# A transformer layer's two feed-forward blocks: one adding transfer, one reload and a few sums made at other places

## The chip, the cores and the metric

The kernel runs on one core of a Trainium2 chip. The metric is the device time of one execution in microseconds (us); lower is better. Three executions of the kernel before took 1108.47, 1108.53 and 1110.59 us, a median of 1108.53.

## What is computed

One layer of a streaming encoder for 512 tokens of width 1024 in float32: a feed-forward block (FFN 1), a mixer (a recurrent branch and windowed attention, joined by gates), and a second feed-forward block (FFN 2). The change touches the two feed-forward blocks alone. Cut to that:

```python
def swiglu(x, w1, w3, w2):
    return (jax.nn.silu(x @ w1) * (x @ w3)) @ w2

f = swiglu(rms_norm(h, ffn1_pre_g[l]), ffn1_w1[l], ffn1_w3[l], ffn1_w2[l])
h = h + 0.5 * rms_norm(f, ffn1_post_g[l])
...
f = swiglu(rms_norm(h, ffn2_pre_g[l]), ffn2_w1[l], ffn2_w3[l], ffn2_w2[l])
h = h + 0.5 * rms_norm(f, ffn2_post_g[l])
```

The hidden width is 2816, that is 22 slices of 128.

## The kernel before

**Precision.** PE multiplies in a short format. Every float32 operand is therefore split into two parts, hi (a rounded copy, by ACT) and lo (the operand less hi, mostly by DVE); `split2` (L211 to L214) does both. Each product is three matmuls: hi by hi, lo by hi, hi by lo. In the rows `whi` and `wlo` are the parts of a weight, and `uT`, `hx` and `hT` hold both parts of an activation.

**Two stages for each block.** Both replace a block matrix product of eight multiplications by one of seven, in which sums and differences of blocks are multiplied.

- `Pairs` computes `x @ w1` and `x @ w3`. Each *pair job* takes two slices of a weight. While job n is multiplied, the operands of job n+1 are prepared: POOL (in FFN 2; POOL and DVE in FFN 1) makes sums of weight blocks, S12 and S34 (L817 to L823), ACT and DVE split them. `late[n, k]` hangs further work on point k of job n. The product of the two halves, `hEO`, is the hidden activation.
- `Halves` computes the hidden activation times `w2` in seven products, m1 to m7, each over G groups of four hidden slices (G is 4 in FFN 1, 5 in FFN 2). A *unit* is one group of one product, twelve matmuls (L651 to L653). FFN 2's order is m1, m5, m2, m6, m3, m7, m4, so units 0 to 4 are m1, 10 to 14 m2, 15 to 19 m6, 20 to 24 m3.

**What sets the order around the change.** The program is written out in the order in which each engine executes it; nothing is reordered later. `Halves.prep` (L594 to L637) prepares a unit up to LEAD = 5 units ahead of its matmuls: it takes two buffers `whi` and `wlo`, has ACT copy the weight to hi (L618), makes lo, splits the activation into `uT` or `hx`, and then calls `sums`, which overwrites blocks in place for later products. There are three ways to make lo: DVE subtracts (L626); or ACT writes a negated copy of the weight (L620) and a DMA issued by POOL adds the weight from memory onto it (L621), as m2 does; or ACT writes a negated copy of hi and the DMA adds the weight from SBUF (L624), for the pairs in BY_ADD. The sums on the weights are named T1 (`b12` less `b11`, needed by m5) and T2, both by `T` (L548, on tiles `raw_w2a` or `raw_w2b`); the sum S1 on the activation is also for m5 (L551, on `hEO`). Each is one DVE instruction. `t1(i)` and `s1(i)` can be called early for a group; `sums` then skips them.

In FFN 2, T1 of groups 0 to 2 stands at `late[end - 2, 1]`, in the job before the last but one; in the trace these are three L548 in a row. S1 of the groups 0 to 3 is early there as well. In FFN 1 neither is early: T1 and S1 of a group stand behind the splits of m1's unit.

m3 uses `b22` again, which T2 has overwritten. In FFN 2 it is loaded a second time, by SP (L633), one DMA for each of five preparations from number `cast_at` on, which is 4 * 5 - 5 = 15. SP's queue is executed in order, and each DMA on it waits until its buffer is free.

Of the kernel before, what the change touches and what calls it, by code (L numbers as in the profile page):

```python
# [51 lines left out]
def hybrid_layer(ctx: ExitStack, tc: tile.TileContext, a: dict, out: bass.AP):  # L52
# [10 lines left out]
    def slot(shape, dt=F32, name="s"):  # L63
        uid[0] += 1
        return sb.tile(shape, dt, tag="slot", name=f"{name}_{uid[0]}")
# [9 lines left out]
    def f32(ap):  # L75
        return ap.bitcast(F32)
# [72 lines left out]
    def dma_to(n):  # L149
        while st["dma"] < min(n, len(order)):  # L150
            dma_one(st["dma"])
            st["dma"] += 1
# [11 lines left out]
    def split_to(n):  # L164
        while st["split"] < min(n, len(order)) and st["split"] not in paired:
            k = st["split"]
            dma_to(k + 1)
            r = raws.pop(k)
            if order[k] in BY_DMA:
                nm, i = order[k]  # L170
                pairs[k] = split_dma(r, a[nm][i * P : (i + 1) * P, :])
            else:
                hi = slot([P, D], F32R, name="whi")
                lo = slot([P, D], F32R, name="wlo")
                if order[k] in BY_POOL:
                    pool.tensor_copy(hi, r)
                else:
                    act.activation(hi, r, AF.Copy)
                dve.tensor_tensor(out=lo, in0=r, in1=f32(hi), op=ALU.subtract)
                pairs[k] = (hi, lo)  # L180
            st["split"] += 1
# [29 lines left out]
    def split2(hi, lo, src):  # L211

        act.activation(hi, src, AF.Copy)  # L213
        dve.tensor_tensor(out=lo, in0=src, in1=f32(hi), op=ALU.subtract)  # L214
# [276 lines left out]
    class Hidden:  # L491

        def __init__(self, seq):
            self.seq, self.f, self.t, self.done, self.eo = seq, {}, {}, 0, {}
# [21 lines left out]
    class Halves:  # L516
# [5 lines left out]
        def __init__(self, nm, hid, hooks, gs, names):  # L522
            self.nm, self.hid, self.hooks, self.gs, self.names = nm, hid, hooks, gs, names
            self.G = G = len(gs)
            self.loads = [(b, i) for bs in (("b11", "b12"), ("b22", "b21")) for i in range(G) for b in bs]
            if G > 4:
                self.loads[2 * G :] = [(b, i) for b in ("b22", "b21") for i in range(G)]
            self.cast_at = names.index("m3") * G - 5
            self.raw, self.ops, self.loaded, self.ready = {}, {}, 0, 0
            self.bank, self.c, self.accs, self.cast, self.did = {}, {}, {}, {}, set()  # L530

# [62 lines left out]
        def prep(self, n, load=True):  # L594

            G = self.G
            while self.ready < min(n, 7 * G):
                u = self.ready
                self.ready += 1
                m, i = self.names[u // G], u % G  # L600
                if load:
                    self.load(min(4 * G, 2 * G + (u if u >= U_SLOTS else u == 3) if G > 4 else 2 * G + 1 + u))
                b, odd, half = self.OPERANDS[m]
                again = m == "m3" and G > 4
                hi = self.cast.pop(i) if m == "m3" and not again else slot([P, 2, 512], F32R, name="whi")
                lo = slot([P, 2, 512], F32R, name="wlo")
                if u < U_SLOTS:
                    xs = slot([P, 2, 2, 256], F32R, name="hx")
                else:
                    xs = uT[:, :, (u + 1) % 8, :].rearrange("p e (j c) -> p e j c", j=2)  # L610
                if again:
                    split2(hi, lo, self.cast.pop(i))
                elif m == "m3":
                    act.activation(lo, f32(hi), AF.Copy, scale=-1.0)
                    pool.dma_start(out=lo, in_=self.src(b, i), accum_op=ALU.add)
                else:
                    src = self.raw[b, i]
                    act.activation(hi, src, AF.Copy)  # L618
                    if m == "m2":
                        act.activation(lo, src, AF.Copy, scale=-1.0)  # L620
                        pool.dma_start(out=lo, in_=self.src(b, i), accum_op=ALU.add)  # L621
                    elif G > 4 and (m, i) in BY_ADD:
                        act.activation(lo, f32(hi), AF.Copy, scale=-1.0)
                        pool.dma_start(out=lo, in_=src, accum_op=ALU.add)  # L624
                    else:
                        dve.tensor_tensor(out=lo, in0=src, in1=f32(hi), op=ALU.subtract)  # L626
                split2(xs[:, 0, :, :], xs[:, 1, :, :], self.x(i, odd, half))
                self.ops[u] = hi, lo, xs
                if self.cast_at <= u < self.cast_at + G:
                    n = u - self.cast_at  # L630
                    if G > 4:
                        self.cast[n] = slot([P, 2, 512], name=f"raw_{self.nm}")
                        sp.dma_start(out=self.cast[n], in_=self.src("b22", n))  # L633
                    else:
                        self.cast[n] = slot([P, 2, 512], F32R, name="whi")
                        pool.dma_start(out=self.cast[n], in_=self.src("b22", n))
                self.sums(m, i)  # L637
# [53 lines left out]
    def blocks(nm, hid, pairs, late, h_src, gs, names, marks):  # L691

        hooks = {u: [] for u in range(7 * len(gs))}

        def tail_tile(n):
            hid.to(n + 1)
            split_to(st["get"] + n + 1)

        def h_back(t):
            h[t] = slot([P, D], name="h")  # L700
            sp.dma_start(out=h[t], in_=h_src(t))

        for at_, fn in zip(marks, (lambda n: dma_to(st["get"] + n + 1), tail_tile, h_back)):
            for n, u in enumerate(at_):
                hooks[u].append(lambda n=n, fn=fn: fn(n))
        half = Halves(nm, hid, hooks, gs, names)
        pairs.more = lambda n: half.load((LOAD_PAIRS if len(gs) == 4 else LOAD_B)[n])
        ahead = lambda: half.prep(min(half.ready + 1, U_SLOTS))
        end = len(pairs.jobs) - 1
        late[end, 1], late[end, 2 if pairs.R is None else 3] = [ahead], [ahead]  # L710
        if pairs.R is None:
            late[end - 4, 1] = [lambda i=i: half.s1(i) for i in range(len(gs) - 1)]
            late[end - 3, 1] = [lambda: half.load(6)]
            late[end - 2, 1] = [lambda i=i: half.t1(i) for i in range(3)]
            late[end - 1, 2] = [lambda: half.prep(1, False)]
            late[end, 1] = []
        pairs.run(ahead, late)
        return half

# [539 lines left out]
    def to_uT(src, hh, th):  # L1259
        v = [uT[:, e, 4 * hh : 4 * hh + 4, th * 256 : th * 256 + 256] for e in range(2)]  # L1260
        split2(v[0], v[1], src)
        return uview(hh, th)
# [19 lines left out]
    def keep(u):  # L1282
        f, i = u // 2, u % 2
        if f not in kept:
            kept[f] = slot([P, 2, SEQ], name="kept")
        act.activation(kept[f][:, i, :], ps[u], AF.Copy)
# [34 lines left out]
    late = {(0, 1): [lambda: keep(2 * NC1 - 1)], (1, 1): [bias_in], (2, 3): [bias_parts], (3, 1): [bias_rows]}  # L1321
# [5 lines left out]

    h.clear()
    half = blocks("w2a", hid, pairs_a, late, lambda t: a["x"][t * P : (t + 1) * P, :], GS_A, NAMES_A, MARKS_A)
    X1 = pairs_a = late = None  # L1330
    for fn, at_ in zip((gate_kept, silu_kept, swiglu_kept), KEPT_AT):
# [5 lines left out]
    half = None  # L1337
# [415 lines left out]
    late = {(0, 1): [lambda: X2.update(t4=to_uT(tn[3], 0, 1)), tn.clear]}  # L1753
    pairs_b.prep(1, 1)

    half = blocks("w2b", hid, pairs_b, late, lambda t: h_scr[t], GS_B, NAMES_B, MARKS_B)
    X2 = pairs_b = None
    last_gemm("w2b", hid, half, "ffn2_post_g", 0.5)
# [106 lines left out]
```

## Time and profile before

| | us |
|---|---|
| median of three executions | 1108.53 |
| the profiled execution | 1108.97 |
| its span in the profile | 1107.2 |
| PE busy | 1096.0 |
| DVE busy | 934.2 |
| ACT busy | 680.1 |
| POOL busy | 407.0 |

The profile shows one execution, instruction by instruction. A row of the timeline has the start, the duration, the engine, the line in the kernel, the operation and the tiles, written as output<-inputs; in brackets, if there is any, the idle time just ahead of it and what ended it. PE is the matmul engine, DVE, ACT and POOL are the vector, scalar and GpSimd engines, SP issues most of the loads. "x3" means that three like instructions are put into one row. Successive matmuls overlap, so that their starts are closer together than their durations are long. PE's granted clock was 0.999 of full speed.

### The profile page before, as it was taken

How to read it: one execution, taken by the hardware profiler on the slowest of the kernel's cores; microseconds unless marked ns; L12 is line 12 of the kernel's file. 1: busy time of each engine (PE TensorE's matmuls, PEld its weight loads, DVE VectorE, ACT ScalarE, POOL GpSimd, SP SyncE). 2: the span in 40 equal slices, each digit the busy share in tenths (PEclk: the TensorE clock that was granted, in tenths of full speed). 3: DMA queues.
4: the chain of work that ended last, by engine and by line, in shares of the span. 5: the costliest groups of instructions: out<-in, count | busy, mean ns of one | idle time of the engine just before them, and what ended most of it. 6: DMA issues, size and time to landing. Idle time of an engine off the chain costs nothing.

```text
span 1107.2 us, 17988 instructions
## 1 busy us (share of the span) xinstructions
PE 1096.0 (99%) x6838; PEld 987.7 (89%) x6838; DVE 934.2 (84%) x1324; ACT 680.1 (61%) x1187; POOL 407.0 (37%) x333
## 2 busy tenths in 40 slices
PE   9999999999999999999999999999999999999997
PEld 8899999987888877899888888888999999998786
DVE  5988999999977978887678867767889899999985
ACT  7755556576747678756656654456455555567672
POOL 0143435602112423233556573010976655521000
PEclk9999999999999999999999999999999999999999
DMA  9325663467944542156222335452323323557742
GB/s 334 124 83 143 132 141 115 133 212 151 250 186 168 149 117 101 39 161 244 72 89 84 112 136 209 138 185 95 116 81 111 115 77 115 190 163 180 190 129 80
DMA packets 53205, 156.44 MB, mean 141 GB/s; under 512 B 5488, under 2 KB 7408, under 8 KB 53120
## 3 DMA queue, kind: packets, MB, share of 16 engines
q1 hardware_dynamic: 44128, 132.19, 35.4%
q0 software_dynamic: 8704, 22.59, 10.5%
q8 instruction: 53, 0.87, 0.3%
q10 hardware_dynamic: 288, 0.52, 0.1%
q14 instruction: 32, 0.26, 0.1%
HBM read 137.47 MB, written 13.62 MB: 136 GB/s over the span
## 4 chain that ended last, share of the span: by engine, by line
PE 89%; DVE 6%; ACT 3%; DMA 1%; issue 1%; DVEq 0%; SPq 0%; ACTq 0%
PE c L770 12%; PE c L771 12%; PE c L769 12%; PE f L224 9%; PE f L226 9%; PE f L225 9%; PE hw L652 5%; PE hw L653 5%; PE hw L651 5%; PE acc L244 1%; PE acc L242 1%; PE acc L243 1%; DVE wlo L214 1%; PE pt L1623 1%; DMA wlo<-in_w2b_dram 1%
## 5 line engine op out<-in xcount | busy, mean ns | idle before, releaser
L770 PE MATMUL c<-uT,wlo 128*128 128x256 f32 x516 | 146.1, 283 | 0.3 <-DVE wlo L214 0.3
L771 PE MATMUL c<-uT,whi 128*128 128x256 f32 x516 | 146.0, 283 | 0.0
L769 PE MATMUL c<-uT,whi 128*128 128x256 f32 x516 | 146.0, 283 | 0.0
L770 PE MATMUL c<-Xh,wlo 128*128 128x256 f32 x504 | 142.9, 284 | 0.7 <-DVE wlo L214 0.5
L769 PE MATMUL c<-Xh,whi 128*128 128x256 f32 x504 | 142.7, 283 | 0.0
L224 PE MATMUL f<-uT,whi 128*128 128x512 f32 (+1 forms) x368 | 136.4, 371 | 0.0
L225 PE MATMUL f<-uT,wlo 128*128 128x512 f32 (+1 forms) x368 | 134.8, 366 | 0.0
L226 PE MATMUL f<-uT,whi 128*128 128x512 f32 (+1 forms) x368 | 134.8, 366 | 0.0
L771 PE MATMUL c<-Xl,whi 128*128 128x256 f32 x456 | 129.0, 283 | 0.0
L214 DVE TENSOR_TENSOR wlo<-S,whi 128x1024 fp32r<-128x1024 f32 x86 | 118.4, 1377 | 5.9 <-POOL OL L1659 3.1
L213 ACT ACTIVATE whi<-S 128x1024 fp32r<-128x1024 f32 x86 | 88.5, 1055 | 33.5 <-DVE S L818 32.1
L770 PEld LDWEIGHTS c<-uT,wlo 128*128 128x128 f32 x516 | 99.0, 192 | 0.7 <-DVE wlo L214 0.5
L769 PEld LDWEIGHTS c<-uT,whi 128*128 128x128 f32 x516 | 99.0, 192 | 0.2
L771 PEld LDWEIGHTS c<-uT,whi 128*128 128x128 f32 x516 | 99.0, 192 | 0.0
L770 PEld LDWEIGHTS c<-Xh,wlo 128*128 128x128 f32 x504 | 96.7, 192 | 1.2 <-DVE wlo L214 1.2
L769 PEld LDWEIGHTS c<-Xh,whi 128*128 128x128 f32 x504 | 96.7, 192 | 0.3 <-issue 0.3
L771 PEld LDWEIGHTS c<-Xl,whi 128*128 128x128 f32 x456 | 87.5, 192 | 0.0
L652 PE MATMUL hw<-wlo,uT 128*128 128x512 f32 x220 | 86.0, 391 | 1.2 <-DMA wlo<-in_w2b_dram 1.1
L653 PE MATMUL hw<-whi,uT 128*128 128x512 f32 x220 | 86.0, 391 | 0.2
L651 PE MATMUL hw<-whi,uT 128*128 128x512 f32 x220 | 85.8, 390 | 0.0
L224 PEld LDWEIGHTS f<-uT,whi 128*128 128x128 f32 x368 | 69.4, 189 | 12.6 <-issue 1.4
L226 PEld LDWEIGHTS f<-uT,whi 128*128 128x128 f32 x368 | 69.4, 188 | 11.4
(440 smaller groups left out, 3183.3 us busy)
## 6 DMA issues: line engine op xcount, KB each, us to landing
raw_w2b<-in_w2b_dram SPq DMA_DIRECT2D x27, 512.0 KB, 4.5
raw_w2a<-in_w2a_dram SPq DMA_DIRECT2D x22, 512.0 KB, 4.3
raw_w1b<-in_w1b_dram SPq DMA_DIRECT2D x22, 512.0 KB, 4.2
raw_w3b<-in_w3b_dram SPq DMA_DIRECT2D x22, 512.0 KB, 4.4
raw_w3a<-in_w3a_dram SPq DMA_DIRECT2D x21, 512.0 KB, 4.4
raw_w1a<-in_w1a_dram SPq DMA_DIRECT2D x20, 512.0 KB, 4.5
raw_wg<-in_wg_dram SPq DMA_DIRECT2D x16, 512.0 KB, 4.2
h<-in_x_dram SPq DMA_DIRECT2D x8, 512.0 KB, 7.3
```

The costliest lines, as they stand in the source:

```text
L213: act.activation(hi, src, AF.Copy)
L214: dve.tensor_tensor(out=lo, in0=src, in1=f32(hi), op=ALU.subtract)
L224: pe.matmul(ps[:, c0:c1], wh[:, s], h_, start=k == 0 and c0 == 0, stop=False, skip_group_check=True)
L225: pe.matmul(ps[:, c0:c1], wl[:, s], h_, start=False, stop=False, skip_group_check=True)
L226: pe.matmul(ps[:, c0:c1], wh[:, s], l_, start=False, stop=k == KT - 1, skip_group_check=True)
L242: pe.matmul(acc[n], x[:, 0, c], wh[:, s], start=first, stop=False, skip_group_check=skip)
L651: pe.matmul(ps, xs[:, 0, j, c], hi[:, j, :], start=start and j == 0, stop=False, skip_group_check=True)
L652: pe.matmul(ps, xs[:, 0, j, c], lo[:, j, :], start=False, stop=False, skip_group_check=True)
L653: pe.matmul(ps, xs[:, 1, j, c], hi[:, j, :], start=False, stop=i == self.G - 1, skip_group_check=True)
L769: pe.matmul(ps, wh[:, s], xh, start=first, stop=False, skip_group_check=True)
L770: pe.matmul(ps, wl[:, s], xh, start=False, stop=False, skip_group_check=True)
L771: pe.matmul(ps, wh[:, s], xl, start=False, stop=k == 3, skip_group_check=True)
```

## The change

Four edits, in three functions.

1. `cast_at` for G = 5 becomes 4 * 5 - 3 = 17: m3's `b22` is reloaded in the preparations 17 to 21.
2. In FFN 2's m2 the lo of group 4 is made by DVE's subtraction (L626) in place of ACT's negated copy and the adding DMA. FFN 1 has four groups and keeps all its adding DMAs.
3. In FFN 2's pair jobs T1 is made early for groups 0 and 1 only. T1(2) is made at its own unit, by `sums`.
4. In FFN 1 (`pairs.R` is not None) S1(0) and S1(1) are made at point 1 of the pair jobs 5 and 9.

```diff
-            self.cast_at = names.index("m3") * G - 5
+            self.cast_at = names.index("m3") * G - (5 if G == 4 else 3)
...
-                    if m == "m2":
+                    if m == "m2" and i < 4:
                         act.activation(lo, src, AF.Copy, scale=-1.0)
                         pool.dma_start(out=lo, in_=self.src(b, i), accum_op=ALU.add)
...
-            late[end - 2, 1] = [lambda i=i: half.t1(i) for i in range(3)]
+            late[end - 2, 1] = [lambda i=i: half.t1(i) for i in range(2)]
             late[end - 1, 2] = [lambda: half.prep(1, False)]
             late[end, 1] = []
+        else:
+            late[5, 1].append(lambda: half.s1(0))
+            late[9, 1].append(lambda: half.s1(1))
```

Where instructions move, on DVE. Lines from 720 on have numbers that are higher by 3 in the changed kernel (L880 and L883 are the same line); the numbers in names are the program's buffers. The first place is FFN 2's pair job ahead of the last but one, before:

```order
L214 TENSOR_TENSOR w22_1918_10381<-raw_w3b19_1882_10126,w22_1918_10381 128x512
L548 TENSOR_TENSOR raw_w2b_1907_10280<-raw_w2b_1907_10280,raw_w2b_1906_10278 128x1024
L548 TENSOR_TENSOR raw_w2b_1909_10284<-raw_w2b_1909_10284,raw_w2b_1908_10282 128x1024
L548 TENSOR_TENSOR raw_w2b_1911_10288<-raw_w2b_1911_10288,raw_w2b_1910_10286 128x1024
L214 TENSOR_TENSOR wlo_1929_10444<-raw_w1b20_1899_10256,whi_1928_10443 128x1024
L214 TENSOR_TENSOR wlo_1931_10461<-S12_1919_10384,whi_1930_10460 128x1024
L880 TENSOR_TENSOR cc_1924_10395<-c_1927_10398,ct_1923_10394 128x256
```

The same place in the changed kernel:

```order
L214 TENSOR_TENSOR w22_1918_10381<-raw_w3b19_1882_10126,w22_1918_10381 128x512
L548 TENSOR_TENSOR raw_w2b_1907_10280<-raw_w2b_1907_10280,raw_w2b_1906_10278 128x1024
L548 TENSOR_TENSOR raw_w2b_1909_10284<-raw_w2b_1909_10284,raw_w2b_1908_10282 128x1024
L214 TENSOR_TENSOR wlo_1929_10443<-raw_w1b20_1899_10256,whi_1928_10442 128x1024
L214 TENSOR_TENSOR wlo_1931_10460<-S12_1919_10384,whi_1930_10459 128x1024
L883 TENSOR_TENSOR cc_1924_10395<-c_1927_10398,ct_1923_10394 128x256
```

The third L548, T1(2) on `raw_w2b_1911`, has gone from ahead of the two splits `wlo_1929` and `wlo_1931`. It now stands in the preparation of m1's unit 2, behind that unit's split of `hx` with two short instructions between it and unit 3's L626.

The second place is in m2, where the fifth group is prepared, before (`uT` from `hEO_1895` is that group's activation, `raw_w2b_1978` and `raw_w2b_1959` are T2 and another sum behind it):

```order
L551 TENSOR_TENSOR hEO_1829_9742<-hEO_1829_9742,hEO_1828_9741 128x2x256
L214 TENSOR_TENSOR uT_78<-hEO_1895_10244,uT_78 128x512
L548 TENSOR_TENSOR raw_w2b_1978_10812<-raw_w2b_1978_10812,raw_w2b_1960_10675 128x1024
L548 TENSOR_TENSOR raw_w2b_1959_10673<-raw_w2b_1978_10812,raw_w2b_1959_10673 128x1024
L551 TENSOR_TENSOR hEO_1895_10244<-hEO_1895_10244,hEO_1894_10243 128x2x256
```

And in the changed kernel:

```order
L551 TENSOR_TENSOR hEO_1829_9742<-hEO_1829_9742,hEO_1828_9741 128x2x256
L626 TENSOR_TENSOR wlo_2009_11016<-raw_w2b_1997_10925,whi_2008_11015 128x1024
L214 TENSOR_TENSOR uT_78<-hEO_1895_10244,uT_78 128x512
L548 TENSOR_TENSOR raw_w2b_1978_10812<-raw_w2b_1978_10812,raw_w2b_1960_10674 128x1024
L548 TENSOR_TENSOR raw_w2b_1959_10672<-raw_w2b_1978_10812,raw_w2b_1959_10672 128x1024
L551 TENSOR_TENSOR hEO_1895_10244<-hEO_1895_10244,hEO_1894_10243 128x2x256
```

The L626 that writes `wlo_2009` is new on DVE; all behind it stands one instruction later.

The third place is FFN 1's last pair job, where m1's first units are prepared, before:

```order
L626 TENSOR_TENSOR wlo_418_2743<-raw_w2a_391_2585,whi_417_2742 128x1024
L214 TENSOR_TENSOR hx_419_2744<-hEO_149_786,hx_419_2744 128x512
L548 TENSOR_TENSOR raw_w2a_392_2587<-raw_w2a_392_2587,raw_w2a_391_2585 128x1024
L551 TENSOR_TENSOR hEO_149_786<-hEO_149_786,hEO_150_787 128x2x256
L912 TENSOR_TENSOR cc_396_2594<-cc_396_2594,Rb_19_144 128x1024
L626 TENSOR_TENSOR wlo_422_2794<-raw_w2a_393_2589,whi_421_2793 128x1024
L214 TENSOR_TENSOR hx_423_2795<-hEO_217_1293,hx_423_2795 128x512
L548 TENSOR_TENSOR raw_w2a_394_2591<-raw_w2a_394_2591,raw_w2a_393_2589 128x1024
L551 TENSOR_TENSOR hEO_217_1293<-hEO_217_1293,hEO_218_1294 128x2x256
```

In the changed kernel both L551 are gone from there. The first now stands in pair job 5:

```order
L895 TENSOR_TENSOR cc_191_1057<-ct_190_1056 128x256
L214 TENSOR_TENSOR w22_201_1168<-raw_w3a9_171_923,w22_201_1168 128x512
L551 TENSOR_TENSOR hEO_149_786<-hEO_149_786,hEO_150_787 128x2x256
L214 TENSOR_TENSOR wlo_212_1213<-raw_w1a10_188_1052,whi_211_1212 128x1024
L915 TENSOR_TENSOR cc_191_1057<-cc_191_1057,Rb_19_144 128x1024
```

The second stands at the like place of pair job 9. On SP the order of the DMAs is unchanged; which buffers m3's reloads take, and so what they wait for, is different.

## Prediction

> **What bounds the kernel now.** I read the page's busy times first, then the waits of the matmul engine, then its rows one by one at the places that the change touches.
>
> ```profile
> span 1107.2 us, 17988 instructions
> PE 1096.0 (99%) x6838; PEld 987.7 (89%) x6838; DVE 934.2 (84%) x1324; ACT 680.1 (61%) x1187; POOL 407.0 (37%) x333
> ```
>
> PE is the bound: it is busy in 1096.0 of 1107.2 us, and the change removes no matmul. So it can win only what PE waits for today. The list of PE's waits is short; its longest entry inside the feed-forward blocks is this one:
>
> ```profile
> PE hw L652 <- DMA wlo<-in_w2b_dram: 1.1, 1, 1.1
> ```
>
> Ends of matmuls are modelled, so a short wait shows better as a gap between starts. In FFN 1's m5 the starts are normally 0.23 us apart (here L653, L651, L652 follow each other):
>
> ```profile
> 249.30 0.39 PE L651 MATMUL hw<-whi,uT 128*128 128x512 f32 x1
> 249.77 0.50 PE L652 MATMUL hw<-wlo,uT 128*128 128x512 f32 x1
> 250.37 0.50 PE L653 MATMUL hw<-whi,uT 128*128 128x512 f32 x1
> 250.71 0.39 PE L651 MATMUL hw<-whi,uT 128*128 128x512 f32 x1
> ...
> 252.78 0.39 PE L651 MATMUL hw<-whi,uT 128*128 128x512 f32 x1
> ...
> 253.85 0.50 PE L653 MATMUL hw<-whi,uT 128*128 128x512 f32 x1
> ```
>
> The first four rows have gaps of 0.47, 0.60 and 0.34, so 0.24 + 0.37 + 0.11 = 0.72 over the normal three. From 252.78 to 253.85 are 1.07 for two steps, 0.61 over. These two units alone lose 1.33 us, and what ends the gaps is DVE, which runs there without a break: its split of uT ends at 253.80, and PE goes on at 253.85.
>
> ```profile
> 253.11 0.69 DVE L214 TENSOR_TENSOR uT<-hEO,uT 128x512 fp32r<-128x512 f32 x1
> ```
>
> **FFN 1: two S1 leave DVE's run.** The run starts in the last pair job:
>
> ```profile
> 226.99 0.68 DVE L551 TENSOR_TENSOR hEO<-hEO,hEO 128x512 f32<-128x512 f32 x1
> ...
> 228.73 1.22 DVE L626 TENSOR_TENSOR wlo<-raw_w2a,whi 128x1024 fp32r<-128x1024 f32 x1
> ...
> 231.60 0.69 DVE L551 TENSOR_TENSOR hEO<-hEO,hEO 128x512 f32<-128x512 f32 x1
> ...
> 232.87 1.22 DVE L626 TENSOR_TENSOR wlo<-raw_w2a,whi 128x1024 fp32r<-128x1024 f32 x1
> ```
>
> Both L551 rows go. Each has 0.69 on the row, but the next instruction starts about 0.09 before the end of the one ahead, so a step is 0.60. ACT's halves of the splits limit how far DVE can move up:
>
> ```profile
> 227.35 1.05 ACT L618 ACTIVATE whi<-raw_w2a 128x1024 fp32r<-128x1024 f32 x1
> ...
> 230.23 1.05 ACT L618 ACTIVATE whi<-raw_w2a 128x1024 fp32r<-128x1024 f32 x1
> ```
>
> The split at 228.73 can't start before 228.40, so the first S1 gives 0.30 there and not 0.60. The one at 232.87 could start at 232.87 - 0.30 - 0.60 = 231.97, after ACT's end at 231.28, so the run is 0.90 early from there. Behind it DVE has no idle time until PE has caught up, and the last gap closes by as much: **-0.90**. Bounds: -0.30 if ACT or a load holds the second split too, -1.33 from PE's gaps.
>
> The same two S1 are added in pair jobs 5 and 9, each ahead of a split that waits for ACT:
>
> ```profile
> 103.97 1.23 DVE L214 TENSOR_TENSOR wlo<-raw_w1a,whi 128x1024 fp32r<-128x1024 f32 x1 [2.62 <-ACT whi L213]
> ...
> 144.29 1.23 DVE L214 TENSOR_TENSOR wlo<-raw_w1a,whi 128x1024 fp32r<-128x1024 f32 x1 [1.18 <-ACT whi L213]
> ```
>
> 0.69 fits into 2.62 and into 1.18: cost 0. That idle time is the cover; without it each would delay its split by 0.60. What lies between FFN 1 and FFN 2 moves with PE.
>
> **FFN 2's pair jobs: one T1 fewer ahead of two splits.** DVE's and POOL's rows, then PE's:
>
> ```profile
> 963.62 4.58 DVE L548 TENSOR_TENSOR raw_w2b<-raw_w2b,raw_w2b 128x1024 f32<-128x1024 f32 x3
> 968.13 2.31 DVE L214 TENSOR_TENSOR wlo<-raw_w1b,whi 128x1024 fp32r<-128x1024 f32 x1
> 970.37 2.31 DVE L214 TENSOR_TENSOR wlo<-S,whi 128x1024 fp32r<-128x1024 f32 x1
> ```
> ```profile
> 967.31 2.05 POOL L822 TENSOR_TENSOR S<-raw_w3b 128x512 f32<-128x512 f32 x1 [2.45 <-PE c L771]
> 969.44 2.15 POOL L823 TENSOR_TENSOR S<-S,raw_w3b 128x512 f32<-128x512 f32 x1
> ```
> ```profile
> 969.94 0.28 PE L769 MATMUL c<-uT,whi 128*128 128x256 f32 x1
> 970.50 0.39 PE L770 MATMUL c<-uT,wlo 128*128 128x256 f32 x1 [0.28 <-DVE wlo L214]
> 970.72 0.28 PE L771 MATMUL c<-uT,whi 128*128 128x256 f32 x1
> ...
> 971.91 0.28 PE L769 MATMUL c<-Xh,whi 128*128 128x256 f32 x1
> 972.73 0.39 PE L770 MATMUL c<-Xh,wlo 128*128 128x256 f32 x1 [0.54 <-DVE wlo L214]
> ```
>
> With 0.12 as the normal step of a 256-wide matmul, PE loses 0.44 before 970.50, 0.70 before 972.73, and 0.10 at each restart (970.50 to 970.72): 1.34 us. The third L548 is T1(2), 1.13 long, and the two splits right behind it end the waits. Without it the first split starts at 967.00, before POOL's addition at 967.31. In the rows the two engines take turns: ends come at 969.36 (POOL), 970.44 (DVE), 971.59 (POOL), 972.68 (DVE), about 1.1 apart, where an undisturbed split takes 1.2. If DVE has its turn first, its splits end at 968.2 and 970.4, and both waits go: **-1.34**. If the splits keep 2.31 each, they end 1.13 early, and PE wins 1.13. So the bounds of this step are 1.13 and 1.34; I take 1.34, because the alternating ends fit the rows one by one. The Trainium skill's page "SBUF — State Buffer", section "Who interferes with whom", calls the port that DVE and GpSimd share an exclusive lock and no split of bandwidth; by that rule the step gives 1.34, by a shared pace 1.13, and the rows' ends agree with the lock.
>
> What is late next is the next job's first split, with 0.38 to spare (981.47 less 981.09):
>
> ```profile
> 979.88 1.21 DVE L214 TENSOR_TENSOR wlo<-raw_w3b,whi 128x1024 fp32r<-128x1024 f32 x1
> ...
> 981.47 0.28 PE L770 MATMUL c<-uT,wlo 128*128 128x256 f32 x1
> ```
>
> POOL's additions wait for PE ahead of the gaps, so they don't move up, and DVE loses some of its lead to them again. By turns, POOL's last addition comes one DVE turn earlier, about 1.1, and DVE's next operation behind it as well: a lead of 1.1 by estimate, 0.24 less than PE's 1.34, inside the 0.38. If DVE had no lead left there, PE would keep only 0.38 of the 1.34.
>
> **FFN 2's m2: the fifth lo by DVE.** In the chain of waits and PE's rows:
>
> ```profile
> 1023.71 8.69 DMA wlo<-in_w2b_dram
> ```
> ```profile
> 1030.98 0.39 PE L651 MATMUL hw<-whi,uT 128*128 128x512 f32 x1
> 1032.44 0.50 PE L652 MATMUL hw<-wlo,uT 128*128 128x512 f32 x1 [1.07 <-DMA wlo<-in_w2b_dram]
> 1032.78 0.39 PE L653 MATMUL hw<-whi,uT 128*128 128x512 f32 x1
> ```
>
> Gaps 1.46 and 0.34 against 0.23: 1.23 + 0.11 = **-1.34**. The adding transfer goes with ACT's negated copy ahead of it; DVE instead makes the lo just ahead of uT's split of the same unit, in a stretch where its splits are done over three us before PE asks for them (3.23 at the least, below). What was behind the transfer on PE needs nothing later than that. Bounds: 0 if something else holds unit 14 as long, 1.34 from PE's rows.
>
> **What DVE then carries.** T1(2) is back at m1's unit 2, a little ahead of the first row here, and the new L626 stands in m2. From here to m3 DVE has no idle time:
>
> ```profile
> 991.55 1.23 DVE L626 TENSOR_TENSOR wlo<-raw_w2b,whi 128x1024 fp32r<-128x1024 f32 x1 [0.38 <-ACT whi L618]
> ...
> 1037.04 0.69 DVE L214 TENSOR_TENSOR uT<-hEO,uT 128x512 fp32r<-128x512 f32 x1
> ```
> ```profile
> 1040.96 0.39 PE L653 MATMUL hw<-whi,uT 128*128 128x512 f32 x1
> ```
>
> The idle 0.38 and the 0.08 of overlap take 0.46 of T1's 1.14; DVE falls 0.68 behind PE. The new L626 adds 1.14, PE's vanished stall 1.34: 3.16 in all. The smallest spare behind it is at unit 17: uT's split ends at 1037.73, PE starts at 1040.96, 3.23, of which 0.06 is the handover. So 3.17 is there for 3.16. DVE becomes the bound's equal; I cost it at nothing, with the upper bound that each us of more lag is a us of PE.
>
> **m3's reload** moves from units 15 to 19 to units 17 to 21 of the preparation.
>
> ```profile
> 1022.83 10.12 SPq L633 DMA_DIRECT2D raw_w2b<-in_w2b_dram  x5
> ```
> ```profile
> raw_w2b<-in_w2b_dram SPq DMA_DIRECT2D x27, 512.0 KB, 4.5
> ```
>
> The five stay in the same place on SP's queue, but by the buffers that they now take they wait for the ends of units 13 to 16, 2.7 us apart (twelve matmuls of 0.23). Unit 16 ends where unit 17 begins, at about 1040.5, less 2.7: the fifth is issued near 1037.8 and lands near 1042.3. It is used in unit 24, seven units behind unit 17, near 1057 in the new time. Cost 0, on ACT's and SP's queues too; the next loads on SP wait for unit 17 and 18 anyway.
>
> **Sum.** 0.90 + 1.34 + 1.34 = 3.58; I write 3.5, since the margin on DVE is 0.01. The profiled execution took 1108.97 (span 1107.2 and 1.77 around it), so 1105.5; the median shown is 0.44 lower, which gives 1105.0. I say **1105.2**.
>
> **Rivals.**
> - *FFN 1 gives 0.30.* ACT's splits or the loads hold DVE. Against it: ACT is 0.7 ahead at 231.28. Sum 2.98: 1105.8.
> - *DVE becomes the bound in m6 or m3.* For it: the margin of 0.01. If the idle time absorbs nothing of T1(2) or POOL takes some tenths, PE loses 0.3 to 1.0 at unit 17 or 20: sum 2.6 to 3.3, 1105.5 to 1106.1.
> - *The next pair job takes T1's gain back, and FFN 1 gives 0.30.* 0.38 + 0.30 + 1.34 = 2.02: 1106.7, no measurable difference. With the m2 lo alone working it is 1107.4.
> - *Slower: the reload.* If SP's five transfers wait for later units than I read, they and the loads behind them slide by 2.7 per unit. The fifth has 1057 less 1042.3, less 2.3 for both halves of its split, 12.4 to spare; slower than before needs 3.6 more, six units in all. That the spare is so large speaks against it; price at eight units: 21.6 - 12.4 - 3.6 = 5.6, 1114.
>
> **Chances.** Forecast 0.50; FFN 1's or DVE's rival, still faster, 0.20; two of them together or the third, within 0.2%, 0.20; slower 0.10. A difference of 0.2%, 2.2 us, is about what a measurement of this kernel tells from none. Low end: 3.58 with PE's full 1.33 in FFN 1, 4.0 below the median, 1104.5; high end: FFN 1's 0.90 or little else works, 1107.9.
>
> **What would show it.** Right: no gap over 0.1 at L652 in m2's last unit; starts 0.12 apart around T1's job; the last m5 gaps of FFN 1 short by 0.9 in sum. Wrong: a wait at L653 on uT in m6 or at L653 of m3's first unit (DVE is the bound), a wait at the next pair job's first L770, a wait on raw_w2b at m3, or L770 waiting in jobs 6 or 10 of FFN 1.

## The result, and the profile after

Ten executions of each kernel: 1108.82 us before (1107.82 to 1111.33), 1106.43 us changed (1105.54 to 1108.23). The ratio is 0.9976, 95% interval 0.9966 to 0.9986: 2.4 us faster. The forecast was 1105.2, in a range of 1104.5 to 1107.9: the measured time lies in it, 1.2 us above the forecast. Of this 1.2, 0.3 is the starting point: the forecast set out from 1108.53, the median of three executions, and the median of ten is 1108.82. The profiled execution of the changed kernel has a span of 1104.3, against 1107.2, that is 2.9 us less. From its page:

```profile
span 1104.3 us, 17988 instructions
PE 1094.8 (99%) x6838; PEld 987.0 (89%) x6838; DVE 935.9 (85%) x1325; ACT 679.3 (62%) x1186; POOL 404.3 (37%) x332
```

One instruction more on DVE, one less on ACT and on POOL, as the order showed. Lines from 720 on are numbered higher by 3 here, so L772 to L774 are the L769 to L771 of before.

To see where the time came from, I set each matmul's start beside the same matmul's start before; where the difference changes, PE has won or lost time. By place, in us (minus is won), forecast and first profile:

| place | forecast | measured |
|---|---|---|
| the kernel's first 20 us (untouched) | 0 | -0.25 |
| FFN 1, m1 and m5 (S1) | -0.90 | -0.91 |
| FFN 1, m3 (untouched) | 0 | +0.71 |
| between, to FFN 2's pair jobs (untouched) | 0 | +0.16 |
| FFN 2's pair jobs (T1) | -1.34 | -1.33 |
| FFN 2's m2 (lo, reload) | -1.34 | -1.37 |
| FFN 2's m6 (DVE) | 0 | +0.09 |
| PE's end, sum | -3.58 | -2.87 |

The list leaves out places with less than 0.05. The three steps came out to 0.03. In FFN 1's m5, of the two units whose gaps the prediction shows, the first has only 0.04 and 0.11 over the normal left of its 0.72, and the second keeps its own (252.10 and 252.70).

```profile
248.73 0.39 PE L651 MATMUL hw<-whi,uT 128*128 128x512 f32 x1
248.95 0.39 PE L652 MATMUL hw<-wlo,uT 128*128 128x512 f32 x1
249.22 0.50 PE L653 MATMUL hw<-whi,uT 128*128 128x512 f32 x1
...
251.64 0.39 PE L651 MATMUL hw<-whi,uT 128*128 128x512 f32 x1
252.10 0.51 PE L652 MATMUL hw<-wlo,uT 128*128 128x512 f32 x1
252.70 0.51 PE L653 MATMUL hw<-whi,uT 128*128 128x512 f32 x1
```

The S1 of pair jobs 5 and 9 lie in DVE's idle time: 0.61 of it is used in each place (2.62 became 2.01, 1.18 became 0.57).

```profile
101.03 0.68 DVE L551 TENSOR_TENSOR hEO<-hEO,hEO 128x512 f32<-128x512 f32 x1
103.73 1.23 DVE L214 TENSOR_TENSOR wlo<-raw_w1a,whi 128x1024 fp32r<-128x1024 f32 x1 [2.01 <-ACT whi L213]
...
142.81 0.67 DVE L551 TENSOR_TENSOR hEO<-hEO,hEO 128x512 f32<-128x512 f32 x1
144.05 1.23 DVE L214 TENSOR_TENSOR wlo<-raw_w1a,whi 128x1024 fp32r<-128x1024 f32 x1 [0.57 <-ACT whi L213]
```

T1's place in FFN 2, DVE's rows and then POOL's:

```profile
963.34 3.45 DVE L548 TENSOR_TENSOR raw_w2b<-raw_w2b,raw_w2b 128x1024 f32<-128x1024 f32 x2
966.71 1.21 DVE L214 TENSOR_TENSOR wlo<-raw_w1b,whi 128x1024 fp32r<-128x1024 f32 x1
967.84 2.31 DVE L214 TENSOR_TENSOR wlo<-S,whi 128x1024 fp32r<-128x1024 f32 x1
```
```profile
967.02 2.06 POOL L825 TENSOR_TENSOR S<-raw_w3b 128x512 f32<-128x512 f32 x1 [2.45 <-PE c L774]
969.15 2.16 POOL L826 TENSOR_TENSOR S<-S,raw_w3b 128x512 f32<-128x512 f32 x1
```

The first split now starts 0.31 ahead of POOL's addition and takes its undisturbed 1.21. POOL's addition, dispatched inside it, ends at 969.08, 1.16 behind the split's end at 967.92; the second split, dispatched inside the addition, ends at 970.15, 1.07 behind that. So one whole turn has gone, 2.24 at the second split's end (972.68 before) with the 0.29 by which everything came earlier taken off, and not the 1.13 of the instruction that was moved. PE's starts have the normal 0.12 at both places:

```profile
969.65 0.28 PE L772 MATMUL c<-uT,whi 128*128 128x256 f32 x1
969.77 0.28 PE L773 MATMUL c<-uT,wlo 128*128 128x256 f32 x1
...
971.09 0.28 PE L772 MATMUL c<-Xh,whi 128*128 128x256 f32 x1
971.21 0.28 PE L773 MATMUL c<-Xh,wlo 128*128 128x256 f32 x1
```

In m2's last unit the 0.23 is back, and at unit 17 DVE is as close as forecast: uT's split ends at 1037.89, PE starts at 1037.97.

```profile
1029.36 0.39 PE L651 MATMUL hw<-whi,uT 128*128 128x512 f32 x1
1029.59 0.39 PE L652 MATMUL hw<-wlo,uT 128*128 128x512 f32 x1
...
1037.97 0.47 PE L653 MATMUL hw<-whi,uT 128*128 128x512 f32 x1
1038.28 0.40 PE L651 MATMUL hw<-whi,uT 128*128 128x512 f32 x1
```
```profile
1037.21 0.68 DVE L214 TENSOR_TENSOR uT<-hEO,uT 128x512 fp32r<-128x512 f32 x1
```

Here the handover of 0.08 was not free: the next start is 0.31 later instead of 0.23, which is the +0.09 of the table.

The loss is in FFN 1's m3. It wasn't touched, but its lo are made by adding transfers, and two of them are waited for, at 291.33 and 297.07 (gaps of 0.50 and 0.40):

```profile
290.83 0.39 PE L651 MATMUL hw<-whi,uT 128*128 128x512 f32 x1
291.33 0.50 PE L652 MATMUL hw<-wlo,uT 128*128 128x512 f32 x1
...
296.67 0.39 PE L651 MATMUL hw<-whi,uT 128*128 128x512 f32 x1
297.07 0.50 PE L652 MATMUL hw<-wlo,uT 128*128 128x512 f32 x1
```

The DMA view of 276 to 300 gives the median time to landing of m3's four adding transfers and of the plain loads beside them, first before, then changed:

```profile
raw_w2a<-in_w2a_dram SPq DMA_DIRECT2D x5, 512.0 KB, 5.5
wlo<-in_w2a_dram POOLq DMA_DIRECT2D x4, 512.0 KB, 9.1
```
```profile
raw_w2a<-in_w2a_dram SPq DMA_DIRECT2D x5, 512.0 KB, 6.1
wlo<-in_w2a_dram POOLq DMA_DIRECT2D x4, 512.0 KB, 10.0
```

Two theories. **A**: the DMA engines are full there, so that these landings stand still while PE moves up, and S1's gain is always given back at m3. **B**: the transfers' time differs from execution to execution, with S1 or without, and this profile caught a longer one.

### The profile page after: what moved, and what is told of

Same layout as the page of the kernel before. It is cut to its first block, busy times and chain, and to the rows that moved or that the text cites. A ratio compares the mean times of both kernels' runs of the same rounds, so it can differ in the third digit from the quotient of the medians.

```text
span 1104.3 us, 17988 instructions
## 1 busy us (share of the span) xinstructions
PE 1094.8 (99%) x6838; PEld 987.0 (89%) x6838; DVE 935.9 (85%) x1325; ACT 679.3 (62%) x1186; POOL 404.3 (37%) x332
## 4 chain that ended last, share of the span: by engine, by line
PE 86%; DVE 7%; ACT 3%; issue 3%; DMA 1%; POOL 0%; DVEq 0%; SPq 0%; POOLq 0%; ACTq 0%
PE c L773 12%; PE c L772 12%; PE c L774 12%; PE f L224 9%; PE f L226 9%; PE f L225 9%; PE hw L652 4%; PE hw L653 3%; PE hw L651 3%; PE acc L244 1%; PE acc L242 1%; PE acc L243 1%; PE pt L1626 1%; DVE raw_w2a L548 1%; DMA wlo<-in_w2a_dram 1%
## 5 line engine op out<-in xcount | busy, mean ns | idle before, releaser
L774 PE MATMUL c<-uT,whi 128*128 128x256 f32 x516 | 146.0, 283 | 0.0
L772 PE MATMUL c<-uT,whi 128*128 128x256 f32 x516 | 146.0, 283 | 0.0
L772 PE MATMUL c<-Xh,whi 128*128 128x256 f32 x504 | 142.7, 283 | 0.0
L774 PE MATMUL c<-Xl,whi 128*128 128x256 f32 x456 | 129.0, 283 | 0.0
L772 PEld LDWEIGHTS c<-uT,whi 128*128 128x128 f32 x516 | 99.0, 192 | 0.2
L774 PEld LDWEIGHTS c<-uT,whi 128*128 128x128 f32 x516 | 99.0, 192 | 0.0
L772 PEld LDWEIGHTS c<-Xh,whi 128*128 128x128 f32 x504 | 96.7, 192 | 0.3 <-issue 0.3
L774 PEld LDWEIGHTS c<-Xl,whi 128*128 128x128 f32 x456 | 87.5, 192 | 0.0
```

The source lines that it names most:

```text
L772: pe.matmul(ps, wh[:, s], xh, start=first, stop=False, skip_group_check=True)
L774: pe.matmul(ps, wh[:, s], xl, start=False, stop=k == 3, skip_group_check=True)
```

## The experiments

Each was timed against the kernel before, whose median was 1109.58 us beside the first four runs and 1109.27 beside the last four. With each comes one profile, so the table at the end shows each place eight more times.

**Each edit alone.** S1 alone:

```diff
+        else:
+            late[5, 1].append(lambda: half.s1(0))
+            late[9, 1].append(lambda: half.s1(1))
```

> Only the edit in FFN 1: S1(0) and S1(1) in pair jobs 5 and 9. Both theories have PE 0.9 us early behind the last gap of m5 (near 250). Theory A, the DMA engines are full while m3's four adding transfers run (280 to 298), so that their landings do not move with PE: the matmuls at 292 and 297 wait, 0.4 to 0.7 us are lost again, and the kernel gains 0.2 to 0.5 us. Theory B, the waits at 292 and 297 in the changed kernel were one execution's chance: the landings move with PE and the kernel gains 0.9 us.

Measured: 1109.02 against 1109.58, ratio 0.9993 (0.9984 to 1.0001), 0.8 us by the ratio but not clear of none. The profile says more: -0.91 in m1 and m5, and nothing lost at m3. The transfers landed 0.8 earlier, with PE 0.9 earlier. So A doesn't hold as a rule.

T1 alone:

```diff
-            late[end - 2, 1] = [lambda i=i: half.t1(i) for i in range(3)]
+            late[end - 2, 1] = [lambda i=i: half.t1(i) for i in range(2)]
```

> Only T1(2) back at its unit. If DVE and POOL take turns: the first split behind the two T1 takes 1.2 us, both of PE's gaps at 970 and 972 go, the step gives 1.34 us and nothing is late behind it (the next job's first split has 0.1 to 0.2 to spare). If the splits kept their 2.31: 1.13. The wait for the adding transfer in m2 stays, at 1.1 to 1.4, since the transfer is issued as much earlier as PE is.

Measured: 1107.56, ratio 0.9981 (0.9972 to 0.9989); -1.33 at the place, as by turns. The expected wait in m2 stayed, but smaller, and this is a second place where an untouched transfer took another time:

```profile
1029.80 0.39 PE L651 MATMUL hw<-whi,uT 128*128 128x512 f32 x1
1030.50 0.50 PE L652 MATMUL hw<-wlo,uT 128*128 128x512 f32 x1 [0.32 <-DMA wlo<-in_w2b_dram]
1030.84 0.40 PE L653 MATMUL hw<-whi,uT 128*128 128x512 f32 x1
```

Gaps of 0.70 and 0.34, 0.58 over the normal, where the profile of before had 1.34. The transfer, from the chain of waits:

```profile
1022.54 7.92 DMA wlo<-in_w2b_dram
```

7.92 instead of 8.69; 7.88 in the run of S1 alone, with 0.54 of gap.

The fifth lo alone:

```diff
-                    if m == "m2":
+                    if m == "m2" and i < 4:
```

> Only the fifth lo of m2 by DVE, with m3's reload at its old preparations 15 to 19. The gap of 1.34 at m2's last unit goes; DVE is 1.14 + 1.34 = 2.48 behind in m6, against 3.17 that are there, so uT's split at unit 17 keeps 0.7 to spare: 1.34 us faster. Rival: the reload needs the later place, and without it something waits in m6 or m3: less than 0.7 us faster.

Measured: 1107.98, ratio 0.9986 (0.9977 to 0.9995), -1.37 at the place and nothing lost in m6 or m3. The reload's later place isn't needed for it.

The reload alone:

```diff
-            self.cast_at = names.index("m3") * G - 5
+            self.cast_at = names.index("m3") * G - (5 if G == 4 else 3)
```

> Only m3's reload in the preparations 17 to 21; the adding transfer of m2's fifth lo stays. Theory: the 8.69 us of that transfer, against about 6.1 of the four ahead of it, came from the reloads on the same DMA engines; with the second reload issued behind it, it lands in 6 to 7 us and the gap of 1.34 shrinks to 0 to 0.3: 1.0 to 1.34 us faster by the reload alone. Rival: the transfer takes 8 to 9 us by itself, or the reload that is left is enough to slow it: no difference, within 0.3 us.

Measured: 1109.27, ratio 0.9992 (0.9983 to 1.0001). In the profile the gap in m2 has gone in full, -1.37, with the adding transfer still in use. It is issued at 1026.50, no plain load is issued between 1009.25 and the first reload at 1028.56, and it takes 6.5 us and lands 0.95 ahead of PE. PE's rows, then SP's reloads, then the times of m2's five adding transfers:

```profile
1033.76 0.39 PE L651 MATMUL hw<-whi,uT 128*128 128x512 f32 x1
1033.99 0.39 PE L652 MATMUL hw<-wlo,uT 128*128 128x512 f32 x1
```
```profile
1028.56 10.97 SPq L633 DMA_DIRECT2D raw_w2b<-in_w2b_dram  x4
```
```profile
DMA to landing us min/median/max: 6.5/7.7/8.8
```

In all five profiles that keep this transfer PE asks for its result 7.5 us after the issue. With the old reload it took 8.69, 7.88 and 7.92, with the later one 6.54 here and 7.38 in the run without the lo below. So moving the reload takes the wait away. That the reloads beside it had made it slow is argued, not shown: another of the five took 8.8 us here with no plain load beside it, so plain loads are not all that makes an adding transfer long. And yet the profiled span is 1108.6, longer than before: FFN 1, which is here as it was before, lost 2.29 at m3.

```profile
298.86 0.39 PE L651 MATMUL hw<-whi,uT 128*128 128x512 f32 x1
300.10 0.50 PE L652 MATMUL hw<-wlo,uT 128*128 128x512 f32 x1 [0.85 <-DMA wlo<-in_w2a_dram]
```
```profile
wlo<-in_w2a_dram POOLq DMA_DIRECT2D x4, 512.0 KB, 10.6
```

That is B, in a kernel without S1. This execution is an extreme one: its span is the longest of the run's eleven, and the others are 1105.8 to 1107.1.

**The changed kernel with one thing different.** Without the lo (the other three edits):

> Three of the four edits: the reload, T1 and S1, while m2's fifth lo stays with the adding transfer. If the later reload alone frees that transfer (6.5 us in the run of the reload alone, 7.9 to 8.7 with the old reload): no gap at m2's last unit, and the time is that of the changed kernel within 0.5 us. If it lands late again once PE is 1.3 us earlier there: PE waits up to 0.5 us, and the kernel is that much slower than the changed one.

Measured: 1107.08, ratio 0.9978 (0.9965 to 0.9990), and -1.27 in m2; the transfer lands 0.11 ahead of PE, which costs 0.05 of a restart. In the profile, reload and lo are two ways to the same 1.3 us; together they don't give it twice. Without the lo, DVE costs nothing in m6. The time is not within the expected 0.5 us, though: it is 1.0 above the 1106.05 of the changed kernel timed beside it, and goes from 1105.60 to 1110.54 where that one goes from 1105.62 to 1106.61. One profile can't show whether the adding transfer that is still there makes this spread.

Without m3's adding transfers in FFN 1:

```diff
                     act.activation(lo, f32(hi), AF.Copy, scale=-1.0)
-                    pool.dma_start(out=lo, in_=self.src(b, i), accum_op=ALU.add)
```

> The changed kernel without the four adding DMAs of FFN 1's m3, so that the weight is not added into lo there. If the lost 0.7 us of the changed kernel's profile came from these transfers: no gap near 291 and 297, S1's 0.9 us kept to the end, a median 0.3 to 1 us below that of the changed kernel and a smaller spread between executions. Rival, the loss has another cause: the gaps stay, no difference to the changed kernel.

This kernel leaves a term out of m3's product, so it is a measurement and no replacement. Measured: 1105.69 (1105.39 to 1106.38), ratio 0.9962 (0.9950 to 0.9974). No gap at m3; PE's end is 3.59 earlier than before. The span is 1103.6. The median is 0.4 below that of the changed kernel timed beside it, with overlapping ranges, and the expected smaller spread didn't show: both spread over 1.0 us in five executions.

With one L626 more on DVE:

```diff
-                    if m == "m2" and i < 4:
+                    if m == "m2" and (i < 4 if G == 4 else i < 3):
```

> The changed kernel with the lo of m2's groups 3 and 4 by DVE, one L626 more. If DVE has no spare in m6 and m3 (0.08 left at unit 17 in the changed kernel's profile): PE waits for uT's split at unit 17 and again at unit 20, 1.0 to 1.1 us in all, and the kernel is 1.1 us slower than the changed one. If DVE still had spare time, no gap there and the same time.

Measured: 1107.67, ratio 0.9981 (0.9973 to 0.9990), 1.6 above the changed kernel timed beside it. In the profile PE loses 1.25 in m6, against 0.12 for that one: 1.13 more, one step of DVE. PE waits at units 16 and 17, not at 20: once it has waited, it is in step.

```profile
1034.72 0.49 PE L652 MATMUL hw<-wlo,uT 128*128 128x512 f32 x1
1035.32 0.50 PE L653 MATMUL hw<-whi,uT 128*128 128x512 f32 x1
...
1038.20 0.50 PE L652 MATMUL hw<-wlo,uT 128*128 128x512 f32 x1
1038.80 0.50 PE L653 MATMUL hw<-whi,uT 128*128 128x512 f32 x1
```

DVE's row at unit 17 ends at 1038.75, right ahead of PE's 1038.80:

```profile
1038.06 0.69 DVE L214 TENSOR_TENSOR uT<-hEO,uT 128x512 fp32r<-128x512 f32 x1
```

The changed kernel once more:

> The changed kernel once more. If the waits of 0.3 to 0.4 us at 291 and 297 belong to the change, they are in this profile too, 0.4 to 0.7 us in all. If they are one execution's chance, they may be gone or larger, from 0 to 2 us, as in the runs before, where FFN 1's m3 lost 0, 0, 0.1 and 2.2 us. FFN 2's three steps must come out as in the first profile, 1.34 and 1.35 within 0.1, and the ratio between 0.997 and 0.998.

Measured: 1106.05 (1105.62 to 1106.61), ratio 0.9964 (0.9952 to 0.9976), 3.2 us faster; that is more than the expected 0.997 to 0.998, though the interval reaches into it. The steps are -0.91, -1.33 and -1.37 again, and m3 of FFN 1 loses nothing:

```profile
291.19 0.39 PE L651 MATMUL hw<-whi,uT 128*128 128x512 f32 x1
291.42 0.39 PE L652 MATMUL hw<-wlo,uT 128*128 128x512 f32 x1
```
```profile
wlo<-in_w2a_dram POOLq DMA_DIRECT2D x4, 512.0 KB, 9.0
```

All profiles, by place, in us against the profile of before:

| run | m1, m5 | FFN 1 m3 | T1 | m2 | m6 |
|---|---|---|---|---|---|
| changed | -0.91 | +0.71 | -1.33 | -1.37 | +0.09 |
| S1 alone | -0.91 | 0.00 | 0.00 | -0.77 | 0.00 |
| T1 alone | -0.02 | +0.19 | -1.33 | -0.76 | 0.00 |
| lo alone | +0.02 | 0.00 | -0.01 | -1.37 | 0.00 |
| reload alone | 0.00 | +2.29 | -0.01 | -1.37 | 0.00 |
| without the lo | -0.91 | +0.45 | -1.33 | -1.27 | 0.00 |
| without m3's additions | -0.87 | 0.00 | -1.33 | -1.37 | +0.11 |
| one L626 more | -0.87 | +0.39 | -1.33 | -1.37 | +1.25 |
| changed again | -0.91 | 0.00 | -1.33 | -1.37 | +0.12 |

The column of FFN 1's m3 is the one that no edit orders: with S1 and the additions 0.71, 0.00, 0.45, 0.39, 0.00, without S1 0.19, 0.00, 2.29, and 0 in the profile of before. The plain loads of the same stretch go with it: their median is 5.3 to 5.6 us in the four profiles that lose nothing there, 5.7 to 6.4 in the five that lose, and 3.8 with the additions out. So in a slow execution both kinds of transfer take longer; which of them slows the other, or what slows both, these profiles don't show.

A profile is one execution, but every timed execution has its span on record, the time from the first to the last instruction. The device time is the span and 1.7 to 2.2 us more in most of them, but up to 4.3 us more in the run of the reload alone. Medians against the kernel before, in us:

| run | device time | span |
|---|---|---|
| S1 alone | -0.6 | -0.8 |
| T1 alone | -2.0 | -2.1 |
| lo alone | -1.6 | -1.4 |
| reload alone | -0.3 | -1.3 |
| without the lo | -2.2 | -2.8 |
| without m3's additions | -3.6 | -3.5 |
| one L626 more | -1.6 | -1.5 |
| changed again | -3.2 | -3.4 |

The reload alone does shorten the work by what its place shows, and its device time hides that outside the span; why, is open. T1 alone gives 0.8 more than its place, as in its profile, where the wait in m2 shrank too. S1, T1 and lo alone make 4.3 in span, and all the edits together 3.4, so the steps are probably not independent: T1's and the lo's may both draw on the wait in m2.

## Why the prediction came out as it did

**S1, -0.90.** Measured -0.87 to -0.91 in six profiles. ACT's end was the limit at the first split, as said (DVE has 0.22 of idle time there now), and nothing held the second. The cover in pair jobs 5 and 9 held.

**T1, -1.34.** Measured -1.33 in six. The choice between the bounds 1.13 and 1.34 fell right, and for the reason given. The Trainium skill's page "SBUF — State Buffer", section "Who interferes with whom", has the shared port as an exclusive lock: the ends at 967.92, 969.08 and 970.15 agree. The next job's first split kept 0.17 to spare where 0.14 was estimated.

**The fifth lo, -1.34.** The mechanism is right, and -1.37 is what the profile of before and the changed ones differ by. The size holds for that profile, though: with the same order of transfers, PE lost 1.34, 0.58 and 0.54 in the three profiles that keep both the adding transfer and the old reload. The median can't gain more than the wait that its executions had.

**DVE as the bound's equal, cost 0.** By the forecast 3.16 of the 3.23 was used and 0.07 left; 0.08 was left. The cost of 0.09 to 0.12 was missed: PE's restart after a close handover. One more L626 turned into 1.13 us of PE, so the upper bound, each us of more lag a us of PE, held there too.

**The reload, cost 0.** Right as a cost, wrong as an account. I looked only for what it might delay, and it had a gain: alone it gives the full step in m2 (-1.37 at the place, -1.3 in the median span), with the adding transfer landing in time. The prediction took 8.69 us of one transfer as given, beside a row that put five loads into the same stretch.

**"What lies between FFN 1 and FFN 2 moves with PE."** This is the step that failed. The sum put nothing on FFN 1's m3, which lies behind m5, or on any place behind it that the change doesn't touch. For the engines that held, but m3 stands on four adding transfers with some 0.5 us to spare, whose time was 9.0 to 10.6 us in the median of four, from one execution to the next. The prediction didn't look at that spare at all, so it was taken as fixed. The loss can't be put down to the change (theory B): it is there without S1, up to 2.29, and absent with it twice. Taken out with the additions, PE's end is 3.59 earlier where the sum was 3.58; the places of the table make 3.46 of it, since m6 costs 0.11, and the rest is from untouched places, so that the last 0.1 of the agreement is luck.

So the forecast of 3.5 was the sum of gaps in one profile, and 2.4 and 3.2 us are what two sets of timed executions gave. The intervals of the two ratios overlap. In the second set the median span is 3.4 shorter than before, and with m3's additions out it is 3.5, so m3 cost little in the typical execution there. In the first set the spans of the changed kernel go from 1103.7 to 1106.4, with a median of 1104.45 against the 1103.9 of the second; that m3's waits vary can make such a difference, but only one of those ten has a profile. Why the transfers' time varies stays open. Of the rivals, FFN 1's smaller gain and the next job's wait didn't occur, DVE as the bound occurred by 0.1, and the reload made nothing wait.

## What to carry to other kernels

A gap that ends with a transfer is a draw from a spread: look at several executions before adding it to a sum, and at what else is on the queues in the same stretch, since moving that may close the gap by itself. What was won from gaps that end with DVE's instructions was the same within 0.04 us in every profile and could be added up. Compare spans as well as device times: a step of 1.3 us showed as 0.3 in the device time. Where two engines take turns, count turns: moving an instruction of 1.13 us brought the second split forward by 2.2.

## What was not expected of the hardware

The first four adding transfers of FFN 2's m2, 512 KB each, took 6.0 to 6.3 us in the profile of before and 6.7 to 8.8 in that of the reload alone; the four of FFN 1's m3, with plain loads beside them, took 5.7 to 12.3 us over all profiles and cost PE between 0 and 2.29 us without any change to them. After a handover with 0.08 us to spare the next matmul's start was 0.08 us late.
